# Where the high parts of expert weights are made, and where gathered rows are turned, in a decoder layer with sixteen experts

## The chip, the cores and the metric

The kernel runs on one core of a Trainium2 chip. The metric is the time of one execution on the device in microseconds (us), the median of several runs. A profile of one execution is there too; its times are in us from the start of its span unless marked ns. Engines are named as in the profile: PE is TensorE's matrix multiply, PEld its weight load, DVE is VectorE, ACT is ScalarE, POOL is GpSimd, SP is SyncE, which here only issues DMAs. A line such as L830 is a line of the kernel before.

## The reference

One layer (DEPTH = 1) over 1024 tokens of width 1024 in float32: forgetting attention with 16 heads, a residual with layer norm, then a mixture of 16 experts with a sigmoid router that gives each token two experts of one group, again a residual with layer norm.

```python
mix = forgetting_attention(h, fox_w_in[j], fox_b_f[j], fox_w_out[j])
h = _layer_norm(ALPHA * h + mix, ln1_g[i], ln1_b[i])
ffn = grouped_moe(h, router_w, router_b, moe_w_gate[i], moe_w_up[i], moe_w_down[i])
h = _layer_norm(ALPHA * h + ffn, ln2_g[i], ln2_b[i])
...
for e in range(N_EXPERTS):
    he = jax.nn.silu(hf @ w_gate[e]) * (hf @ w_up[e])
    y = y + combine[:, e:e + 1] * (he @ w_down[e])
```

Each expert has three weight matrices: gate and up of 1024 x 512, down of 512 x 1024, 2 MB each in float32.

## The kernel before

**Precision.** A float32 operand is kept as two float16 parts, high and low; a product is three matmuls (`mm3`, L93 to L97: high by high, high by low, low by high). `split` (L65) makes the parts of weights: the high part with a scaled copy on ACT (L68) or on POOL (L70), the low part as scaled source minus high part on DVE (L71). The low part is the last reader of the raw tile.

**Stages.** Value projection, then attention over eight pairs of heads, output projection with first layer norm and router (`out_units`, `route`), then the experts, then the last normalizations and the scatter of the result. Expert 0's weights are loaded during the output projection.

**The expert stage.** `JOBS` is a list of (expert, first slot, slots): expert 0 in two jobs of 80 slots, all others in one of 160, computed as a part of 128 rows and one of 32. The loop in `run` (L1331 to L1368) does for job q: `gather` of job q+1, `load_chunk` of its three weight matrices, up-projections `up` of job q for blocks f = 1 to 3, `up` of job q+1 for f = 0, `rows` of job q-1, `down` of job q.

- `load_chunk` (L757) brings a matrix in four chunks of 128 x 1024 float32 (512 KB) through five raw buffers. Tiles `mh0`, `mh1`, `mh2` are the high parts of gate, up and down, `ml0` to `ml2` the low parts; suffix a or b is the parity of the expert, so two experts' weights are held. High parts alternate between ACT and POOL (L786), except for expert 1, where all are on ACT.
- `gather` (L814) fetches a part's rows (high and low halves of 1024 columns each, float16) from DRAM by an indirect DMA from POOL into `xg`, and turns them into `xT` with the token index in the free dimension: 16 column blocks of 128. For the part of 128 rows the first eight blocks are turned by a DMA transpose issued from SP (L825); the other eight, and all 16 of the part of 32 rows, by TensorE against an identity (L829), eight blocks to a PSUM tile `xq`, and copied to `xT` by DVE (L830). The tag `tp` has two PSUM buffers.
- `up` computes gate and up products for a block of 128 hidden units (L833 to L842, 48 matmuls into `gu`), then tanh on ACT (L857), two DVE operations `a` and `t` (L858, L859), the high half of the hidden values on ACT (L860) and the low half on POOL (L861).
- `down` multiplies with the down weights; the large part is copied with its gate on ACT (`yr`, L896) and added into `acc` in DRAM by an indirect DMA from POOL (L940). The small part goes through `yl` on ACT (L930) and the sum `yT` on DVE (L931), is turned back in `rows` of the next job and added likewise.

**Order.** Each engine works through its own queue in order, and a wait holds everything behind it. The order in a queue is laid down when the program is built, from priorities, and need not be that of the text; `issue_after(ins)` asks that the instructions of its block on the engine of `ins` come behind `ins` in that engine's queue. `self.turned` holds, in the expert stage, the last copy into `xT` that `gather` issued; before, the same name also held sets of finished blocks of the attention.

Of the kernel before, what the change touches and what calls it, by code (L numbers as in the profile page):

```python
# [21 lines left out]
NT, KT, NP = S // 128, D // 128, H // 2  # L22
# [4 lines left out]
WS = 64.0  # L27
# [7 lines left out]
NA, CA, TA = 1, 80, 5  # L35
# [23 lines left out]
class Kern:  # L59
# [18 lines left out]
    def fill(self, us):  # L78
        done = 0
        while us > done and self.fill_q:  # L80

            at = next((n for n, u in enumerate(self.fill_q) if len(u) < 3 or u[2] in self.turned[NP - 1]), None)
            if at is None:
                break
            c, f = self.fill_q.pop(at)[:2]
            f()
            done += c
        return done
# [296 lines left out]
    def attn_o(self, hp, i, j, pT, ps):  # L385
        nc, wk = self.nc, self.wk
        hd = 2 * hp + j
        nb = QG if hp < NP - 1 else 1
        if i % nb == 0 and j == 0:
            self.o_ps = ps.tile([128, QG, 2, HD + 1], F32, name="ops", bufs=2)  # L390
        V = self.V[hd // 8]
        vo = hd % 8 * VW
        vh, vl = slice(vo, vo + HD + 1), slice(vo + HD + 2, vo + VW)
        o = self.o_ps[:, i % nb, j, :]
        for b in range(i + 1):
            nc.tensor.matmul(o, pT[:, b, :], V[b][:, vh], start=(b == 0), stop=False)  # L396
            nc.tensor.matmul(o[:, :HD], pT[:, b, :], V[b][:, vl], start=False, stop=False)  # L397
            nc.tensor.matmul(o, pT[:, i + 1 + b, :], V[b][:, vh], start=False, stop=(b == i))  # L398
        if j == 0 or i % nb < nb - 1:
            return  # L400
        T = self.o_ps[:, :nb]
        r = wk.tile([128, QG, 2, 1], F32, name="ro", bufs=2)[:, :nb]
        nc.vector.reciprocal(r, T[:, :, :, HD:])
        x = wk.tile([128, QG, 2, HD], F32, name="ox", bufs=1)[:, :nb]
        nc.vector.tensor_tensor(x, T[:, :, :, :HD], r.to_broadcast([128, nb, 2, HD]), op=OP.mult)  # L405
        sg = self.SG[hp, i // 4].rearrange("p (a b c) -> p a b c", b=2, c=HD)[:, (i + 1 - nb) % 4:i % 4 + 1]
        self.gated = nc.gpsimd.tensor_tensor(x, x, sg, op=OP.mult)  # L407
        gh, gl = (wk.tile([128, QG, 2, HD], F16, name=f"g{n}", bufs=2)[:, :nb] for n in "hl")
        nc.scalar.activation(gh, x, AF.Copy)
        nc.gpsimd.tensor_tensor(gl, x, gh, op=OP.subtract)  # L410
        ts = slice((i + 1 - nb) * 128, (i + 1) * 128)
        def turn():
            for g, oT in ((gh, self.oTh), (gl, self.oTl)):
                nc.sync.dma_start_transpose(oT[:, hp, ts].rearrange("p (a b) -> p a b", b=128),
                                            g.rearrange("p a b c -> p (a b c)"))
            self.turned[hp].add(i)
        self.later.append((self.now + 2, turn))

    def pairs(self, ps):
# [337 lines left out]
    def load_chunk(self, n):  # L757
        e, kind = divmod(n, 3)
        nc, I = self.nc, self.I
        if kind == 2:  # L760
            src = I["moe_w_down"][0, e].rearrange("(k p) c -> p k c", p=128)
            shape = [128, FT, D]
        else:
            src = I[("moe_w_gate", "moe_w_up")[kind]][0, e].rearrange("(k p) c -> p k c", p=128)
            shape = [128, KT, DE]
        pool, sfx = (self.p3a, "a") if e % 2 == 0 else (self.p3b, "b")
        h = pool.tile(shape, F16, name=f"mh{kind}{sfx}")
        l = pool.tile(shape, F16, name=f"ml{kind}{sfx}")
        nk = 1024 // shape[2]
        for c in range(shape[1] // nk):  # L770
            if n == 3 * NA:

                if c % 2 == 0:
                    both = self.p3b.tile([128, 2, nk, shape[2]], F32, name="raww", tag=("mh2b", "ml2b")[c // 2])
                r = both[:, c % 2]
            else:
                r = self.p3a.tile([128, nk, shape[2]], F32, name="raw", tag="raw", bufs=5)
            ks = slice(c * nk, (c + 1) * nk)
            nc.sync.dma_start(r, src[:, ks, :])
            self.sp_n += 1  # L780
            if e == NA:
                with self.tc.issue_after(self.exp.ins), self.tc.issue_after(self.indexed.ins):
                    self.split(h[:, ks, :], l[:, ks, :], r, WS, "act")
            else:
                with self.tc.issue_after(self.turned.ins) if e == 2 and 4 * kind + c >= 4 else ExitStack():
                    self.split(h[:, ks, :], l[:, ks, :], r, WS, ("act", "pool")[self.sp_n % 2 if e != 1 else 0])  # L786
        self.MW[n] = (h, l)


# [24 lines left out]
    def gather(self, job):  # L814
        nc = self.nc
        e, jo, jn = job
        xT = self.p3b.tile([128, 2 * KT, CAP], F16, name="xT", bufs=2)[:, :, :jn]
        for q, (o, n) in enumerate(self.parts(job)):
            xg = self.p3b.tile([128, 2 * D], F16, name=f"xg{q}", bufs=2)
            idx = self.idx[o]  # L820
            self.got = nc.gpsimd.indirect_dma_start(  # L821
                out=xg[:n, :], out_offset=None, in_=self.hl_d,
                in_offset=bass.IndirectOffsetOnAxis(ap=idx[:n, e:e + 1], axis=0))
            if n > 64 and e >= NA:
                nc.sync.dma_start_transpose(xT[:, :8, o - jo:o - jo + n], xg[:n, :8 * 128])  # L825
            for c in range(8 if n > 64 and e >= NA else 0, 2 * KT, 8):
                p = self.psr.tile([128, 8, n], F16, name="xq", tag="tp", bufs=2)
                for k in range(8):
                    nc.tensor.transpose(p[:, k, :], xg[:n, (c + k) * 128:(c + k + 1) * 128], self.identh[:n, :n])  # L829
                self.turned = (nc.vector.tensor_copy if e >= NA else nc.scalar.copy)(xT[:, c:c + 8, o - jo:o - jo + n], p)  # L830
        self.XT[job] = xT

    def up_mm(self, gu, job, f):  # L833
# [436 lines left out]
    def run(self):  # L1270
        tc, nc, I = self.tc, self.nc, self.I
        self.w_k = I["fox_w_in"].rearrange("a d c -> (a d) c").rearrange("(k p) c -> p k c", p=128)
        self.W, self.QA, self.SG = {}, {}, {}
        self.turned = [set() for _ in range(NP)]
        self.wo, self.OP = [None, None], {}
        self.wo_k = I["fox_w_out"].rearrange("a (k p) c -> p (a k) c", p=128)
        self.LR, self.FR, self.ROOM, self.YT, self.p2b, self.MW, self.XG, self.XT, self.sp_n = {}, {}, [], {}, None, {}, {}, {}, 0
# [107 lines left out]
```

## Time and profile before

| | |
|---|---|
| runs | 1164.64, 1170.14, 1173.2 us; median 1170.14 us |
| profiled execution | 1179.74 us, its span 1177.9 us |
| mean granted TensorE clock | 0.932 of full speed |
| busy: PE, DVE, ACT, POOL | 995.7, 798.1, 523.9, 444.1 us |
| DMA queue of SP and ACT, and of POOL | 62.3% and 10.4% of 16 engines' span |

Busy shares are means over stages with different limits; the rows below cut the expert stage out and divide it into periods, one per expert. A row of waits tells how long an engine stood idle and which instruction ended that.

### The profile page before, as it was taken

The numbers are of one execution on the slowest core, as the hardware profiler recorded it, in microseconds if no ns is written. First come the engines' busy times: TensorE is split into PE (matmuls) and PEld (weight loads), VectorE is DVE, ScalarE is ACT, GpSimd is POOL, SyncE is SP. The second block draws the span as 40 slices with busy tenths as digits, with TensorE's granted clock in tenths as the row PEclk, the third lists the DMA queues.
The fourth block names the chain that finished last, engine by engine and source line by source line (L and its number), as shares of the span: only waits on it lengthen the run. The fifth ranks groups of instructions, "written<-read, shape, count | busy, mean of one in ns | idle before, by whom it ended". The sixth has DMA issues, their size and how long they took to land. (4 is left out here: it accounts for less than half of the span.)

```text
span 1177.9 us, 27374 instructions
## 1 busy us (share of the span) xinstructions
PE 995.7 (85%) x11246; PEld 703.0 (60%) x11246; DVE 798.1 (68%) x1408; ACT 523.9 (44%) x835; POOL 444.1 (38%) x438
## 2 busy tenths in 40 slices
PE   7799799999989998978789778889789888888860
PEld 3344466575765756554344666777677767776740
DVE  3423566767667786747499768767986767777765
ACT  4111456657666575735053544433343434443431
POOL 3400421222222322123110146666665666554453
PEclk9899899999999999989899979988989999989985
DMA  8900285778678687668776479999899999998560
GB/s 247 229 19 1 53 130 110 142 131 142 126 130 155 139 166 139 121 140 149 197 253 228 164 202 304 311 278 274 246 294 262 289 265 284 280 277 258 154 204 37
DMA packets 290467, 221.77 MB, mean 188 GB/s; under 512 B 207640, under 2 KB 232216, under 8 KB 290336
## 3 DMA queue, kind: packets, MB, share of 16 engines
q1 hardware_dynamic: 281120, 188.50, 62.3%
q0 software_dynamic: 8640, 29.37, 10.4%
q8 instruction: 90, 1.47, 0.5%
q10 hardware_dynamic: 576, 2.10, 0.4%
q14 instruction: 41, 0.34, 0.1%
HBM read 147.80 MB, written 23.69 MB: 146 GB/s over the span
## 5 line engine op out<-in xcount | busy, mean ns | idle before, releaser
L379 DVE SCALAR_TENSOR_TENSOR hl<-s,hl 128x256 f16<-128x256 f32 (+7 forms) x128 | 102.0, 797 | 83.6 <-ACT hl L378 81.9
L376 ACT ACTIVATE s<-sp,mn 128x256 f32<-128x256 f32 (+7 forms) x128 | 94.3, 737 | 90.0 <-DVE mn L374 88.1
L407 POOL TENSOR_TENSOR ox<-ox,sg 128x256 f32<-128x256 f32 (+1 forms) x36 | 32.0, 888 | 252.5 <-DVE ox L405 252.5
L374 DVE TENSOR_REDUCE mn<-sp 128x1 f32<-128x256 f32 (+7 forms) x128 | 95.2, 749 | 14.5 <-PE sp L372 13.4
L95 PE MATMUL pj<-xTh,wh 128*128 128x512 f16 x256 | 97.9, 382 | 7.1 <-ACT qa L351 7.1
L378 ACT ACTIVATE hl<-s 128x256 f16<-128x256 f32 (+7 forms) x128 | 87.3, 682 | 25.8 <-DMA pT<-hl 22.9
L97 PE MATMUL pj<-xTh,wl 128*128 128x512 f16 x256 | 97.8, 382 | 0.0
L96 PE MATMUL pj<-xTl,wh 128*128 128x512 f16 x256 | 97.8, 382 | 0.0
L95 PE MATMUL pj<-wh,xTh 128*128 128x128 f16 x512 | 92.5, 225 | 1.0 <-POOL wh L70 1.0
L96 PE MATMUL pj<-wl,xTh 128*128 128x128 f16 x512 | 92.5, 225 | 0.0
L97 PE MATMUL pj<-wh,xTl 128*128 128x128 f16 x512 | 92.5, 225 | 0.0
L940 POOL DMA_INDIRECT acc<-yr,dst x29 | 56.0, 1931 | 72.1 <-DMA raw<-in_moe_w_gate_dram 26.3
L95 PEld LDWEIGHTS <-xTh 128*128 128x128 f16 x704 | 69.5, 100 | 21.5 <-DMA xTh<-xhl 3.7
L96 PEld LDWEIGHTS <-xTh 128*128 128x128 f16 x704 | 69.3, 100 | 17.9 <-issue 3.2
L97 PEld LDWEIGHTS <-xTl 128*128 128x128 f16 x704 | 69.3, 100 | 16.9 <-issue 2.6
L396 PE MATMUL ops<-v,pT 128*128 128x65 f16 x576 | 66.9, 194 | 14.0 <-DMA pT<-hl 14.0
L860 ACT ACTIVATE hh<-t 128x160 f16<-128x160 f32 (+1 forms) x68 | 22.1, 327 | 127.1 <-DVE t L859 126.8
L369 PE MATMUL sp<-kx,qa 128*128 128x512 f16 (+2 forms) x192 | 62.4, 325 | 17.5 <-ACT s L376 17.1
L396 PEld LDWEIGHTS <-pT 128*128 128x128 f16 x576 | 54.5, 98 | 29.8 <-DMA pT<-hl 19.5
L397 PE MATMUL ops<-v,pT 128*128 128x64 f16 x576 | 67.0, 196 | 0.0
L398 PE MATMUL ops<-v,pT 128*128 128x65 f16 x576 | 66.6, 194 | 0.0
L821 POOL DMA_INDIRECT xg<-hl_d,idx x31 | 49.7, 1605 | 40.2 <-DVE gsum L706 18.0
(369 smaller groups left out, 3513.9 us busy)
## 6 DMA issues: line engine op xcount, KB each, us to landing
raw<-in_moe_w_up_dram SPq DMA_DIRECT2D x64, 512.0 KB
raw<-in_moe_w_down_dram SPq DMA_DIRECT2D x64, 512.0 KB
raw<-in_moe_w_gate_dram SPq DMA_DIRECT2D x60, 512.0 KB
wr<-in_fox_w_in_dram SPq DMA_DIRECT2D x48, 256.0 KB
xr<-in_x_dram SPq DMA_DIRECT2D x8, 512.0 KB
xh<-in_x_dram SPq DMA_DIRECT2D x16, 256.0 KB
wvr<-in_fox_w_in_dram SPq DMA_DIRECT2D x6, 512.0 KB
hl_d<-hlr SPq DMA_DIRECT2D x6, 512.0 KB
```

Of the source, the lines that this page charges most:

```text
L95: nc.tensor.matmul(p, ah, bh, start=first, stop=False)
L96: nc.tensor.matmul(p, ah, bl, start=False, stop=False)
L97: return nc.tensor.matmul(p, al, bh, start=False, stop=last)
L369: nc.tensor.matmul(sp[:, ks], self.QA[hp][:, j, qb], self.KX[hp % 2][:, 2 * j, ks], start=True, stop=False)
L374: self.mn = nc.vector.tensor_reduce(mn, sp[:, :n], axis=AX, op=OP.min)
L376: nc.scalar.activation(s[:, :n], sp[:, :n], AF.Exp, scale=-1.0, bias=mn)
L378: nc.scalar.activation(hl[:, :n], s[:, :n], AF.Copy, scale=PS)
L379: nc.vector.scalar_tensor_tensor(hl[:, n:], s[:, :n], PS, hl[:, :n], op0=OP.mult, op1=OP.subtract)
L396: nc.tensor.matmul(o, pT[:, b, :], V[b][:, vh], start=(b == 0), stop=False)
L397: nc.tensor.matmul(o[:, :HD], pT[:, b, :], V[b][:, vl], start=False, stop=False)
L398: nc.tensor.matmul(o, pT[:, i + 1 + b, :], V[b][:, vh], start=False, stop=(b == i))
L940: self.nc.gpsimd.indirect_dma_start(out=self.acc, out_offset=bass.IndirectOffsetOnAxis(ap=self.dst[self.key(job, o)][:n, job[0]:job[0] + 1 ...
```

## The change

For all experts the high part of every weight chunk is made on ACT. In `gather` the DMA transpose goes; all 16 column blocks of either part are turned on TensorE, in two PSUM tiles of eight. The copies out of PSUM, four per expert, are shared: of the part of 128 rows the first on DVE and the second on ACT, of the part of 32 rows the first on ACT and the second on DVE. `issue_after(self.turned.ins)`, before for expert 2 alone (chunks from up chunk 0 on), now also holds for experts 3 to 15, for down chunks 1 to 3. The sets of the attention get a name of their own, `turns`.

```diff
@@ load_chunk
             else:
-                with self.tc.issue_after(self.turned.ins) if e == 2 and 4 * kind + c >= 4 else ExitStack():
-                    self.split(h[:, ks, :], l[:, ks, :], r, WS, ("act", "pool")[self.sp_n % 2 if e != 1 else 0])
+                with self.tc.issue_after(self.turned.ins) if e >= 2 and 4 * kind + c >= (4 if e == 2 else 9) else ExitStack():
+                    self.split(h[:, ks, :], l[:, ks, :], r, WS, "act")
@@ gather
-            if n > 64 and e >= NA:
-                nc.sync.dma_start_transpose(xT[:, :8, o - jo:o - jo + n], xg[:n, :8 * 128])
-            for c in range(8 if n > 64 and e >= NA else 0, 2 * KT, 8):
+            for c in range(0, 2 * KT, 8):
                 p = self.psr.tile([128, 8, n], F16, name="xq", tag="tp", bufs=2)
                 for k in range(8):
                     nc.tensor.transpose(p[:, k, :], xg[:n, (c + k) * 128:(c + k + 1) * 128], self.identh[:n, :n])
-                self.turned = (nc.vector.tensor_copy if e >= NA else nc.scalar.copy)(xT[:, c:c + 8, o - jo:o - jo + n], p)
+                self.turned = (nc.vector.tensor_copy if e >= NA and (c == 0) == (n > 64) else nc.scalar.copy)(xT[:, c:c + 8, o - jo:o - jo + n], p)
```

The other three hunks only rename `turned` to `turns` in `fill`, `attn_o` and `run`.

## Rows read from the trace of the kernel before

**Rows 1.** page, slices of the span; one digit for each fortieth, busy tenths
```profile
PE   7799799999989998978789778889789888888860
...
DMA  8900285778678687668776479999899999998560
```

**Rows 2.** windows of 13 expert periods: us, busy (count) by engine, clock, DMA share, GB/s
```profile
957.16:986.27 29.11, 24.55 (x315) 20.82 (x315) 20.97 (x25) 11.21 (x21) 17.30 (x15) 0.94 0.99 278
...
1044.19:1070.48 26.29, 22.34 (x312) 19.00 (x310) 20.03 (x22) 9.16 (x16) 12.79 (x10) 1.00 0.98 273
sum 375.96, PE 320.52 PEld 273.13 DVE 277.67 ACT 141.81 POOL 228.44; mean PE 24.66 PEld 21.01 DVE 21.36 ACT 10.91 POOL 17.57
```

**Rows 3.** waits of TensorE, 694 to 1071 us: total, times, longest
```profile
PE xq L829 <- DVE xT L830: 29.1, 10, 4.4
```

**Rows 4.** windows around a gap of TensorE
```profile
1002.00:1004.00 2.00, 0.71 (x13) 0.67 (x13) 1.90 (x5) 1.24 (x2) 0.00 (x0) 0.94 0.97 254
1004.00:1006.00 2.00, 2.00 (x18) 2.00 (x16) 0.77 (x2) 0.00 (x0) 0.00 (x0) 0.50 0.80 289
```

**Rows 5.** windows around three DMA transposes, and one of weights alone
```profile
962.00:965.00 3.00, 3.00 (x16) 1.34 (x15) 2.60 (x4) 1.25 (x2) 0.00 (x0) 1.00 1.32 144
990.00:993.00 3.00, 3.00 (x17) 1.51 (x16) 2.90 (x4) 1.25 (x2) 0.06 (x1) 1.00 1.23 217
1019.00:1022.00 3.00, 3.00 (x15) 1.35 (x14) 3.00 (x6) 0.47 (x2) 0.00 (x0) 1.00 1.27 119
...
1025.00:1029.00 4.00, 3.61 (x93) 3.32 (x92) 4.00 (x5) 2.42 (x5) 3.28 (x3) 1.00 1.04 397
```

**Rows 6.** groups by line, 640 to 1178 us: busy, mean ns, idle before
```profile
L71 DVE SCALAR_TENSOR_TENSOR ml2b<-raw,mh2b 128x1024 f16<-128x1024 f32 x32 | 45.1, 1437 | 27.7 <-POOL mh2b L70 21.3 <-ACT mh2b L68 6.4
...
L71 DVE SCALAR_TENSOR_TENSOR ml2a<-raw,mh2a 128x1024 f16<-128x1024 f32 x28 | 37.3, 1365 | 26.4 <-POOL mh2a L70 24.6 <-ACT mh2a L68 1.8
...
L68 ACT ACTIVATE mh2b<-raw 128x1024 f16<-128x1024 f32 x18 | 19.0, 1056 | 28.4 <-DMA raw<-in_moe_w_down_dram 25.0 <-SPq L1145 3.3
...
L70 POOL TENSOR_SCALAR mh2b<-raw 128x1024 f16<-128x1024 f32 x14 | 18.2, 1555 | 0.6 <-DMA raw<-in_moe_w_down_dram 0.6
...
L603 ACT COPY hT<-tp 128x1024 f16<-128x1024 f16 x5 | 4.9, 1014 | 4.7 <-PE tp L602 4.7
```

**Rows 7.** groups by line and form on ScalarE, 724 to 1071 us
```profile
L860 ACT ACTIVATE hh<-t 128x160 f16<-128x160 f32 x48 | 16.0, 336 | 104.3 <-DVE t L859 104.3
...
L68 ACT ACTIVATE mh2a<-raw 128x1024 f16<-128x1024 f32 x13 | 13.7, 1057 | 25.0 <-DMA raw<-in_moe_w_down_dram 25.0
...
L68 ACT ACTIVATE mh1a<-raw 128x1024 f16<-128x1024 f32 x12 | 12.6, 1049 | 6.3 <-DMA raw<-in_moe_w_up_dram 6.3
```

**Rows 8.** timeline of GpSimd, one period: start, us, instruction, idle before
```profile
978.22 1.58 POOL L940 DMA_INDIRECT acc<-yr,dst  x1 [5.48 <-DMA raw<-in_moe_w_gate_dram]
979.28 2.61 POOL L70 TENSOR_SCALAR mh2b<-raw 128x1024 f16<-128x1024 f32 x2
```

**Rows 9.** timeline of VectorE, the same period
```profile
974.28 0.88 DVE L830 COPY xT<-xq 128x1024 f16<-128x1024 f16 x2
976.44 1.23 DVE L71 SCALAR_TENSOR_TENSOR ml2b<-raw,mh2b 128x1024 f16<-128x1024 f32 x1 [1.28 <-ACT mh2b L68]
977.58 0.28 DVE L830 COPY xT<-xq 128x256 f16<-128x256 f16 x1
980.92 4.33 DVE L71 SCALAR_TENSOR_TENSOR ml2b<-raw,mh2b 128x1024 f16<-128x1024 f32 x3 [3.05 <-POOL mh2b L70]
```

**Rows 10.** timeline of SyncE's queue, the same period
```profile
973.86 10.65 SPq L779 DMA_DIRECT2D raw<-in_moe_w_gate_dram  x4
```

**Rows 11.** groups by line and form, 957.16 to 986.27 us
```profile
L829 PE MATMUL xq<-identh,xg 128*128 128x128 f16 x8 | 0.6, 219 | 0.0
```

**Rows 12.** windows of the stage that loads expert 0
```profile
600.00:620.00 20.00, 18.58 (x154) 9.04 (x152) 19.97 (x38) 11.04 (x12) 1.50 (x1) 1.00 0.75 258
```

**Rows 13.** DMA queues, 700 to 1050 us: packets, MB, share
```profile
q0 software_dynamic: 4496, 15.34, 20.8%
```

More of the change, by code (lines that the diff above doesn't have):

```diff
@@ L80, in fill @@
         while us > done and self.fill_q:
-            at = next((n for n, u in enumerate(self.fill_q) if len(u) < 3 or u[2] in self.turned[NP - 1]), None)
+            at = next((n for n, u in enumerate(self.fill_q) if len(u) < 3 or u[2] in self.turns[NP - 1]), None)
             if at is None:
@@ L415, in turn @@
                                             g.rearrange("p a b c -> p (a b c)"))
-            self.turned[hp].add(i)
+            self.turns[hp].add(i)
         self.later.append((self.now + 2, turn))
@@ L1273, in run @@
         self.W, self.QA, self.SG = {}, {}, {}
-        self.turned = [set() for _ in range(NP)]
+        self.turns = [set() for _ in range(NP)]
         self.wo, self.OP = [None, None], {}
```

## The prediction, written before the result was known

> **What bounds the kernel now.** I read the page's slices first, then windows by stage. From the 25th of the 40 slices on (about 700 us) the experts run one after another; there the DMA row stands at 9, twice at 8, up to the 37th slice, while TensorE (PE) mostly shows 8. The tail, with TensorE at 6 and then 0, is final normalization that the change does not touch [rows 1]. So the expert stage is to be priced. I cut it at the issues of the DMA transpose, one per expert: 13 periods in 375.96 us, 28.92 us each. Their sum row gives per period TensorE 24.66 busy, VectorE (DVE) 21.36, ScalarE (ACT) 10.91, GpSimd (POOL) 17.57; the DMA share is 0.99 and 0.98 in the two periods shown [rows 2].
>
> Two things are nearly full at once. The DMA engines hardly pause. TensorE has 24.66 us of work, part of it at the lower of its two clock levels: the one period with a granted clock of 1.00 needed 22.34 us and lasted only 26.29 [rows 2]. Of TensorE's idle 4.26 us per period, 29.1 us in 13 periods (2.2 each) is a wait for DVE's copy of a transposed block (xT, L830) [rows 3]; the rest, 2.0, are waits for links of the activation. No wait of TensorE names a weight tile, so weights bound the stage indirectly: their splits sit in the in-order queues of DVE, ACT and POOL ahead of the copies that TensorE does wait for. An idle gap is followed by half clock: 0.94 in the two microseconds with the gap, 0.50 in the two behind it [rows 4]. So a period is 22.34 work + 4.26 idle + 2.32 lower clock.
>
> **The change part by part.**
>
> *DMA transposes out.* Fifteen go, one per expert from expert 1 on. In three windows of 3 us around one, the DMA engines moved 144, 217 and 119 GB/s; in 4 us of weights alone 397 [rows 5]. A transpose carries 128x1024 values of 2 bytes, 0.262 MB. In the first window 0.432-0.262 = 0.170 MB of other data moved, worth 0.43 us at 397 GB/s: 2.57 us were lost. The others give 2.02 and 2.76 by the same sum. I take the mean, 2.45 us per period, and keep 2.02 and 2.76 as bounds. The first two of the fifteen lie before the periods, where I count nothing: 13 x 2.45 = 31.9 us.
>
> The Trainium skill says otherwise: its page "Advanced Engine Details and Errata", section "X-Bar Transpose (TRN2)", holds that transpose DMAs are as fast as regular ones. By that, the 0.262 MB would cost what as many bytes of weights cost. The windows speak against it, so it is only a rival below.
>
> *Splits from POOL to ACT.* POOL loses 90 high parts, six for each expert but expert 1, in groups that average up to 1.56 us; ACT gains as many at 1.06 us [rows 6]: +6.3 us per period. ACT also takes two of the four copies of transposed blocks: one 128x1024 PSUM read, nearest row 1.01 us (hT) [rows 6], and one 128x256, nearest row hh of 128x160, 0.34 [rows 7]. ACT then has 10.9+6.3+1.4 = 18.6 us of work in 26 to 29: hidden, as long as what it waits for does not add up.
>
> What the move removes is a queue effect. In one period POOL stood 5.48 us before it could issue an accumulate into acc at 978.22, and only then made two high parts of the down weights [rows 8]; DVE idled 3.05 us for them and did three low parts from 980.92 to 985.25 [rows 9]; raw buffers come free with DVE's low parts, and SP needed 10.65 us to issue four gate loads [rows 10]. Altogether DVE waited 24.6 and 21.3 us for POOL's down parts, 3.3 us per expert [rows 6]. How much of this shortens the period the trace does not show: nothing if the DMA engines stay full anyway, 3.3 at most. Below zero is possible too, since all high parts now stand in one queue with tanh and hh; the nearest price is ACT's average wait for a raw tile, 83.7 us in the six L68 rows (first and last shown) over 73 splits, 1.15 us [rows 7]. With a DMA share near 1 I stay close to zero: a gain of 0.5 us per period, 6.5 us in all.
>
> DVE's low parts also get faster. Alone an L71 takes 1.23 us; the three beside POOL took 4.33, 1.44 each [rows 9], and the six groups average 1.42 (the two for down weights 1.37 and 1.44) [rows 6]. Twelve per expert at 1.23 save 2.3 us, and one 128x256 copy goes to ACT: DVE falls to about 18.8 us. This is slack, not a term.
>
> *Eight more TensorE transposes per expert.* A group of eight 128x128 was busy 0.6 us [rows 11]. It lies beside TensorE's idle unless that vanishes, so I cost it at nothing, and raise TensorE's floor to 22.34+0.6 = 22.9. The blocks share two PSUM buffers: block 3 waits for copy 1 (DVE; two copies of 128x1024 and 128x256 took 0.88 us [rows 9]), block 4 now for copy 2 (ACT, 1.01). Best case some 1 us of waiting in all, a floor of 23.9, against 2.2 us of waiting now. The next up matmuls are queued behind these transposes.
>
> *The order edge.* For experts from 3 on, the low parts of down chunks 1 to 3 on DVE must follow the last copy. In the trace they already do: copy at 977.58, those three at 980.92 [rows 9]. I cost it at nothing; SP would pay, whose gate loads wait for those raw buffers. SP's queue loses a transpose issue and its wait for the gather.
>
> *Expert 0's load* (six splits) goes to ACT, which in that stage was busy 11.04 of 20 us while DVE was full, 19.97 [rows 12]. POOL's six splits become six of 1.06 us on an ACT with room for them: nothing, bounds -1 (DVE without POOL beside it) and +3 us (half of the six in the way).
>
> **Sum.** 2.45 + 0.5 = 2.95 us per period, 25.97 instead of 28.92; 13 periods give 38.4 us. Cross-check from TensorE: 22.9 work + 1.0 for the copies + 1.5 other idle + 0.6 lower clock = 26.0. The profiled execution took 1179.74 us, its span 1177.9; the median of the three runs is 1170.14, 9.6 lower. I take the difference off the median: 1132 us, or 1141 for a profiled one like this.
>
> **Rivals.**
> 1. *More than the sum.* The period falls to TensorE's floor, 23.9: 13 x 5.0 = 65 us, 1105. For it: a period of 26.29 us exists already, with a DMA transpose in it. Against: DMA needs 6.29 MB of weights at 397 GB/s, 15.9 us, plus the software queue's 20.8% of 350 us over 12.1 periods, 6.0 [rows 13]: 21.9 of 23.9 with five raw buffers.
> 2. *A DMA transpose costs no more than plain bytes.* Then 0.262 MB at 397 GB/s is 0.66 us; with 0.5: 13 x 1.16 = 15 us, 1155. The skill's rule named above is this one; the windows of 119 and 144 GB/s are against it.
> 3. *The wait moves, nothing is won.* Copy 1 still stands on DVE behind the sum yT, which needs ACT's yl, and ACT now has two more up parts ahead of yl. TensorE's 2.2 us for xT and the half clock stay, the freed DMA time goes unused: 1158 to 1178, about 1168. For it: copy 1 ran only at 974.28 [rows 9], when TensorE had long finished its block.
> 4. *Slower: ACT as the serial queue.* Copies 2 and 3 on ACT are queued behind high parts that wait for raw tiles, and TensorE waits for copy 2. Price: one average raw wait, 1.15, plus the 0.6 of new transposes, 1.75 x 13 = 23 us: 1193. It decides once TensorE's wait for xT per period exceeds 2.2-0.6 = 1.6 us with the clock unchanged and the DMA gain unused. For it: in twelve periods ACT waited 104.3 us for t and 83.7 for raw tiles [rows 7], 15.7 per period; with 18.6 of work that would make 34. Against: waits behind POOL's late parts are among the longest of these, and they go.
>
> **Chances.** Forecast (1110 to 1150) 0.58, rival 1 0.08, rival 2 0.08, rival 3 0.14, rival 4 0.12. A measurement of this kernel tells about 1%, 12 us, from no change. Faster by over 1%: 0.58 + 0.08 + 0.06 of rival 2: 0.72. Within 1%: the rest of rival 2 and rival 3, 0.16. Slower: 0.12. The range leaves out rival 4 and part of rival 3: 1103 to 1166. The bounds fit: the transpose's 2.02 to 2.76 move the time by +6 to -4 us, the queue effect's -1.15 to 3.3 by +21 to -36, where TensorE's floor cuts in at 1105, and expert 0's load by +3 to -1.
>
> **What will show it.** Right: periods near 26 us; no 3 us windows under 150 GB/s where the transposes were; no DVE wait for POOL at L71 and L71 near 1.23 us; TensorE's wait for xT near 1 us per period; a granted clock above 0.95. Wrong: ACT's waits for t or raw tiles grow, TensorE waits for ACT's copies of xT, or the DMA share falls with the period unchanged, which would say that the DMA engines were not the bound.

## The result and the profile after

The changed kernel takes 1127.2 us (median of 4 runs, 1124.01 to 1128.11) against 1171.67 for the kernel before (1164.64 to 1175.1): a ratio of 0.96, 95% interval 0.9568 to 0.9632. The forecast was 1132, its range 1103 to 1166. The profiled execution took 1126.3 us, its span 1124.5.

The page's slices of the kernel after. Against [rows 1], TensorE shows 9 through most of the expert stage, and the DMA row is as full as it was:

```profile
PE   7899799999999898997789978899999999989860
...
DMA  9900176678577987667768547999999999999551
```

DMA transposes no longer mark the periods, so from here on a period runs from one start of the sum yT on VectorE to the next (L931 before, L929 after), 14 of them in each kernel. Windows over these 14, kernel before; columns as in [rows 2]:

```profile
742.90:1143.00 400.10, 337.68 (x4365) 288.23 (x4364) 291.98 (x458) 154.31 (x283) 236.62 (x186) 0.92 0.91 263
```

The same of the kernel after:

```profile
734.00:1089.50 355.50, 327.01 (x4482) 279.37 (x4479) 254.77 (x443) 239.29 (x384) 137.42 (x113) 0.96 0.92 286
```

Divided by 14, the period went from 28.58 to 25.39 us. VectorE's work in it went from 20.9 to 18.2 (18.8 forecast), ScalarE's from 11.0 to 17.1 (18.6 forecast), GpSimd's from 16.9 to 9.8; the clock went from 0.92 to 0.96. Of the 53.4 us between the two profiled executions (1179.74 and 1126.3), 14 x 3.19 = 44.6 lie here. Another 8.9 lie ahead of the first period, as its start moved from 742.9 to 734.0; the profiled execution of before was itself 8 us above its median. In all eight profiled executions that make expert 0's high parts on ScalarE alone, those of the experiments below among them, the first sum comes at 732.9 to 738.9 us; in the three that alternate for all of them (742.9, 745.3 and 740.5) it comes later, and in the two that alternate for a part between (736.2 and 737.4). So some of this start belongs to expert 0's load. From the end of the periods to the end of the span it is 34.9 and 35.0.

TensorE's waits in the 14 periods after (us, times, longest). In the 14 periods before it stood 32.2 us for xT; [rows 3] has 29.1 for 13:

```profile
PE xq L827 <- DVE xT L828: 13.0, 8, 2.9
...
PE xq L827 <- ACT xT L828: 0.9, 2, 0.6
```

Groups by line after, 640 to 1124 us; they answer to [rows 6]:

```profile
L71 DVE SCALAR_TENSOR_TENSOR ml2b<-raw,mh2b 128x1024 f16<-128x1024 f32 x32 | 37.9, 1221 | 9.1 <-ACT mh2b L68 9.1
...
L71 DVE SCALAR_TENSOR_TENSOR ml2a<-raw,mh2a 128x1024 f16<-128x1024 f32 x28 | 33.5, 1222 | 6.2 <-ACT mh2a L68 6.2
...
L68 ACT ACTIVATE mh2b<-raw 128x1024 f16<-128x1024 f32 x32 | 32.7, 1055 | 8.9 <-DMA raw<-in_moe_w_down_dram 8.7
```

The waits for GpSimd are gone. For the down parts, what VectorE waits for ScalarE in their place is much less: 9.1 and 6.2 us instead of 27.7 and 26.4. For the gate parts it waits longer than before (15.9 and 12.5 us instead of 11.9 and 11.1); over all six tiles 58.2 us are left of 88.6. The low parts all take 1.22 to 1.23 us. VectorE's timeline in one period shows it, beside the gap of 3.05 us and the 4.33 us for three low parts in [rows 9]:

```profile
910.52 0.42 DVE L929 TENSOR_TENSOR yT<-yp,yl 128x256 f32<-128x256 f32 x1 [0.22 <-ACT yl L928]
910.86 0.68 DVE L828 COPY xT<-xq 128x1024 f16<-128x1024 f16 x1
911.47 1.23 DVE L71 SCALAR_TENSOR_TENSOR ml2a<-raw,mh2a 128x1024 f16<-128x1024 f32 x1
...
913.58 2.36 DVE L71 SCALAR_TENSOR_TENSOR ml2a<-raw,mh2a 128x1024 f16<-128x1024 f32 x2 [0.50 <-ACT mh2a L68]
```

ScalarE, with six microseconds more to do per period, waits less. Its waits in the 14 periods after, first for t, then for a raw tile; [rows 7] has 104.3 and 25.0 us in twelve periods:

```profile
ACT hh L858 <- DVE t L857: 31.7, 28, 2.7
...
ACT mh2a L68 <- DMA raw<-in_moe_w_down_dram: 2.6, 5, 1.0
```

Over all six rows of its high parts the wait for raw tiles went from 77.3 to 40.8 us in the 14 periods.

So the signs that the prediction named came true: periods near 26 us, no wait of VectorE for GpSimd, low parts at 1.22, a wait for xT near 1 us per period (0.9, and 0.06 more for ScalarE's copies), a clock above 0.95 in the stage. Whether they came for the reasons given is another matter.

### The profile page after: what moved, and what is told of

Same layout as the page of the kernel before. It is cut to its first block, busy times and chain, and to the rows that moved or that the text cites. A ratio compares the mean times of both kernels' runs of the same rounds, so it can differ in the third digit from the quotient of the medians.

```text
span 1124.5 us, 27572 instructions
## 1 busy us (share of the span) xinstructions
PE 988.6 (88%) x11366; PEld 698.4 (62%) x11366; DVE 751.5 (67%) x1393; ACT 625.9 (56%) x955; POOL 321.9 (29%) x348
## 5 line engine op out<-in xcount | busy, mean ns | idle before, releaser
L407 POOL TENSOR_TENSOR ox<-ox,sg 128x256 f32<-128x256 f32 (+1 forms) x36 | 31.9, 887 | 253.2 <-DVE ox L405 253.2
L859 POOL TENSOR_TENSOR hh<-t,hh 128x160 f16<-128x160 f32 (+1 forms) x56 | 54.5, 975 | 150.7 <-ACT hh L858 150.6
L95 PE MATMUL pj<-wh,xTh 128*128 128x128 f16 x512 | 92.1, 224 | 1.0 <-POOL wh L70 1.0
L938 POOL DMA_INDIRECT acc<-yr,dst x29 | 49.2, 1696 | 74.0 <-ACT mh2b L68 17.9
L95 PE MATMUL gu<-xT,mh0a 128*128 128x160 f16 (+1 forms) x288 | 58.9, 235 | 3.6 <-DVE t L857 3.6
```

Of the source, the lines that this page charges most:

```text
L95: nc.tensor.matmul(p, ah, bh, start=first, stop=False)
L859: (nc.vector if e >= E - 2 or (e < NA and jo == 0) else nc.gpsimd).tensor_tensor(hl[:, f, :], t, hh[:, f, :], op=OP.subtract))
```

## The experiments

Two readings stand against each other. The prediction's: the DMA transposes fill the engines that bound the stage, and taking them out makes most of the gain; the splits give little. Its rival: the stage waits for the split weights, GpSimd is late and slow with its high parts, and taking the splits from it makes the gain, while full DMA engines are not the bound. Each result is given with its ratio to the kernel before, run on the same chip. The kernel before has medians of 1171.67 to 1174.85 us on the chips used, so a difference in us to the kernel after, which was run apart from the experiments, is good to about 3 us.

**1. The splits alone.** All high parts go to ScalarE; DMA transposes, copies and order edge are as before.

```diff
--- after
-  with self.tc.issue_after(self.turned.ins) if e >= 2 and 4 * kind + c >= (4 if e == 2 else 9) else ExitStack():
+  with self.tc.issue_after(self.turned.ins) if e == 2 and 4 * kind + c >= 4 else ExitStack():
...
-            for c in range(0, 2 * KT, 8):
+            if n > 64 and e >= NA:
+                nc.sync.dma_start_transpose(xT[:, :8, o - jo:o - jo + n], xg[:n, :8 * 128])
+            for c in range(8 if n > 64 and e >= NA else 0, 2 * KT, 8):
...
-  self.turned = (nc.vector.tensor_copy if e >= NA and (c == 0) == (n > 64) else nc.scalar.copy)(...)
+  self.turned = (nc.vector.tensor_copy if e >= NA else nc.scalar.copy)(...)
```

> The changed kernel with the DMA transposes and DVE copies of the kernel before and without the new order edge: only the splits are moved to ACT. Theory of the prediction (the DMA transposes carry most of the gain, 31.9 of 38.4 us): about 6.5 us under the kernel before, 1165, the period near 28.4 us. Rival (POOL's late high parts are the main loss, 3.3 us per expert): 13 x 3.3 = 43 us under it, about 1129, equal to the changed kernel.

Measured: 1139.56 us, 0.9692 (0.9651 to 0.9732), 35.3 us below the kernel before. The 14 periods:

```profile
734.50:1103.40 368.90, 327.19 (x4365) 280.89 (x4364) 258.81 (x458) 227.73 (x359) 124.51 (x112) 0.94 0.96 286
```

A period is 26.35 us, 2.2 less than before, with every DMA transpose still in it. Three quarters of the gain come from the part that the prediction priced at 6.5 us.

**2. The turning alone.** TensorE turns all blocks and ScalarE makes half of the copies; high parts alternate as before.

```diff
--- after
-  with self.tc.issue_after(self.turned.ins) if e >= 2 and 4 * kind + c >= (4 if e == 2 else 9) else ExitStack():
-      self.split(h[:, ks, :], l[:, ks, :], r, WS, "act")
+  with self.tc.issue_after(self.turned.ins) if e == 2 and 4 * kind + c >= 4 else ExitStack():
+      self.split(h[:, ks, :], l[:, ks, :], r, WS, ("act", "pool")[self.sp_n % 2 if e != 1 else 0])
```

> The changed kernel with splits alternating between ACT and POOL and without the new order edge: only the turning of the column blocks is moved to TensorE. Theory of the prediction: 13 x 2.45 = 31.9 us under the kernel before, about 1140. Rival (a transpose costs what plain bytes cost, 0.66 us): 9 us under it, about 1163. If this and the splits alone add up to the 44.5 us between the two kernels, the parts are independent; if both fall short, one needs the other.

Measured: 1180.13 us, 1.0042 (1.0019 to 1.0064): no gain, half a per cent slower. The 14 periods:

```profile
745.30:1151.50 406.20, 346.66 (x4487) 295.17 (x4486) 290.13 (x443) 169.13 (x308) 222.09 (x186) 0.91 0.82 250
```

The DMA share falls from 0.91 to 0.82 and the period does not get shorter (29.01). That is the very sign for which the prediction said it would mean that the DMA engines were not the bound. What stays is TensorE's wait for the copies (32.2 us before, here 23.3 for VectorE's and 10.3 for ScalarE's) and VectorE's wait for GpSimd, 45.9 us for the two down tiles in the 14 periods before, here 56.1:

```profile
DVE ml2b L71 <- POOL mh2b L70: 28.5, 7, 5.4
DVE ml2a L71 <- POOL mh2a L70: 27.6, 6, 6.4
```

**3. Which of the splits.** In the kernel before, once only the down parts (2 of GpSimd's 6) go to ScalarE, once only gate and up (4 of 6). If the cost is the place in GpSimd's queue behind the accumulate, the first should give most of it; if it is the time that GpSimd runs beside VectorE, the second.

```diff
--- before
-  ("act", "pool")[self.sp_n % 2 if e != 1 else 0]
+  ("act", "pool")[self.sp_n % 2 if e != 1 and kind != 2 else 0]
```

> The kernel before with the high parts of the down weights alone on ACT; gate and up still alternate. It keeps 4 of the 6 POOL splits of an expert. Theory A (the loss is POOL's queue: down parts stuck behind the accumulate): most of the 35 us that the splits alone gave, 1142 to 1150. Theory B (the loss is each split beside DVE, by shared time or by POOL's slower split): a third of it, 12 us, 1160 to 1165.

```diff
--- before
-  ("act", "pool")[self.sp_n % 2 if e != 1 else 0]
+  ("act", "pool")[self.sp_n % 2 if e != 1 and kind == 2 else 0]
```

> The kernel before with the high parts of gate and up all on ACT; down still alternates. It keeps 2 of the 6 POOL splits of an expert. Theory A (POOL's queue behind the accumulate): at most 10 us of the 35, 1165 to 1175. Theory B (each split beside DVE costs): two thirds, 23 us, about 1150.

Measured: 1149.42 us, 0.9805 (0.9766 to 0.9843), and 1148.46, 0.9789 (0.9753 to 0.9825): 23.6 and 24.5 us, the same within their intervals. VectorE's waits in the 14 periods with down on ScalarE, and then with gate and up there:

```profile
DVE ml0b L71 <- POOL mh0b L70: 14.1, 6, 4.2
DVE ml0a L71 <- POOL mh0a L70: 12.8, 6, 3.4
```

```profile
DVE ml2b L71 <- POOL mh2b L70: 15.7, 6, 3.6
DVE ml2a L71 <- POOL mh2a L70: 13.3, 5, 4.6
```

Neither reading holds alone. Each half brings two thirds of the 35 us, so the halves overlap: whichever stays on GpSimd keeps a wait (3.0 and 2.1 us per period, of 5.2). That either half relieves the one queue that both share would explain it; no run shows that by itself.

**4. GpSimd busy beside VectorE, with nobody waiting for it.** In the kernel after, GpSimd scales every second high part into a tile that nothing reads. This adds work and leaves the outputs as they are.

```diff
--- after
      self.split(h[:, ks, :], l[:, ks, :], r, WS, "act")
+     e > 1 and self.sp_n % 2 and nc.gpsimd.tensor_scalar(
+         self.p3b.tile([128, 8, 128], F16, name="junk", bufs=1), ..., WS, 1.0, op0=OP.mult, op1=OP.mult)
```

> The changed kernel with a scaling of 128x1024 on POOL for every second chunk of experts from 2 on, from the high part into a tile that nobody reads: POOL is as busy beside DVE as before, but no split waits for it. Theory A (POOL's queue order was the loss): 0 to 8 us over the changed kernel, 1127 to 1135, although L71 grows to 1.4 us. Theory B (running beside DVE was the loss): 20 to 35 us more, 1147 to 1162.

Measured: 1144.44 us, 0.9765 (0.9727 to 0.9802), 17 above the kernel after and between the two forecasts. Groups by line, 640 to 1137 us:

```profile
L71 DVE SCALAR_TENSOR_TENSOR ml0b<-raw,mh0b 128x1024 f16<-128x1024 f32 x28 | 48.2, 1736 | 7.7 <-ACT mh0b L68 7.7
...
L71 DVE SCALAR_TENSOR_TENSOR ml2b<-raw,mh2b 128x1024 f16<-128x1024 f32 x32 | 42.5, 1359 | 8.3 <-ACT mh2b L68 8.3
...
L787 POOL TENSOR_SCALAR junk<-mh0b 128x1024 f16<-128x1024 f16 x14 | 23.7, 1690 | 3.7 <-ACT mh0b L68 3.3
```

The low parts, 1.22 us in the kernel after, take 1.36 to 1.74. The 14 periods:

```profile
733.90:1103.80 369.90, 328.01 (x4481) 279.24 (x4478) 301.83 (x444) 240.94 (x384) 245.35 (x189) 0.96 0.90 276
```

VectorE's work is 21.6 us per period instead of 18.2, and the period 26.42 instead of 25.39: the slower low parts are no slack, as the prediction had called them. About a third as much as their 3.4 us ends up in the period. But the slower low parts are not all of it. The extra scalings also stand in GpSimd's own queue, ahead of the low half of the hidden values (hh), for which TensorE waits. TensorE's waits in the 14 periods, here and then in the kernel after:

```profile
PE yp L886 <- POOL hh L859: 8.2, 7, 1.6
```

```profile
PE yp L886 <- POOL hh L859: 1.1, 3, 0.4
```

These 7.1 us are half of the 13.4 us by which TensorE's idle grew (28.5 to 41.9 us). No split waits for GpSimd here, but TensorE does, and the run does not part the two.

**5. A DMA transpose put back.** First the transpose of the gathered rows, into a tile that nothing reads, beside TensorE's own. It stands in SyncE's queue and waits there for the gather.

```diff
--- after
+            if n > 64 and e >= NA: nc.sync.dma_start_transpose(
+                self.p3b.tile([128, 8, 128], F16, name="xd", bufs=1), xg[:n, :8 * 128])
             for c in range(0, 2 * KT, 8):
```

> The changed kernel with the DMA transpose of the first eight column blocks added back into a tile that nobody reads; TensorE still turns all blocks. It prices the transpose (with its place in SP's queue) where the DMA engines are full and the splits no longer wait for POOL. Theory now (the splits were the limit, the transpose costs its lost transfer time only once they are out of the way): between the 12 us by which the splits alone fall short of the changed kernel and 13 x 2.45 = 31.9 us; 1139 to 1159. Rival (it costs what plain bytes cost): 9 us, 1136 or less.

Measured: 1168.35 us, 0.9963 (0.9942 to 0.9984), 41 above the kernel after: nearly the whole gain, and more than either forecast. SyncE's waits, 690 to 1040 us:

```profile
SPq L823 <- DMA xg<-hl_d,idx: 92.1, 10, 10.0
```

Ten waits of 9 us each, with the weight loads queued behind them. This mixes the transfer with the wait. A second kernel was meant to part them: it transposes a high part of the previous expert, which was taken to be long ready, again into a tile that nothing reads, 14 times.

```diff
--- after
   p = self.psr.tile([128, 8, n], F16, name="xq", tag="tp", bufs=2)
+  c == 0 and n > 64 and e > NA and nc.sync.dma_start_transpose(
+      self.p3b.tile([128, 8, 128], F16, name="xd", bufs=1),
+      self.MW[3 * (e - 1)][0][:, 0:2, :].rearrange("p a b -> p (a b)"))
```

> The changed kernel with one DMA transpose of 128x1024 per expert from 2 on that waits for nothing late: its source is the gate high part of the expert before, its target is read by nobody. It prices the transfer alone, without SP waiting for a gather. Theory (2.45 us of lost transfer time each, the DMA engines being full now): 14 x 2.45 = 34 us at most, 1150 to 1161. Rival 1 (plain bytes, 0.66 us): 9 us, 1136. Rival 2 (the DMA engines still have slack, the 41 us of the transpose that waited for its gather were SP's wait): 0 to 5 us, 1127 to 1132.

Measured: 1143.56 us, 0.9744 (0.9679 to 0.9808): 16.4 above the kernel after, 1.2 us for each transpose, and none of the three forecasts. The 14 periods:

```profile
734.10:1105.00 370.90, 332.44 (x4474) 285.25 (x4473) 256.10 (x443) 241.19 (x384) 130.16 (x113) 0.94 0.97 283
```

The source was not ready, though: the loads are issued so far ahead that the transpose reaches the head of SyncE's queue before ScalarE has made that high part. One case, the high part on ScalarE and the transpose in SyncE's queue:

```profile
879.63 2.01 ACT L68 ACTIVATE mh0b<-raw 128x1024 f16<-128x1024 f32 x2
```

```profile
880.71 1.71 SPq L825 DMA_TRANSPOSE xd<-mh0b  x1
```

SyncE's waits there, 640 to 1180 us, the first two of four rows that add up to 58.6 us:

```profile
SPq L825 <- ACT mh0a L68: 24.7, 4, 7.3
SPq L825 <- ACT mh0b L68: 15.8, 3, 6.1
```

So the 1.2 us hold a wait too, and bound what the transfer alone costs from above. The kernel with the transpose of the gathered rows has 114.8 us of such waits by the same view and takes 24.8 us longer for 56.2 us more of waiting; at that rate (an estimate) the 58.6 us of waiting alone could account for all of the 16.4 us. No run has the transfer without a wait.

What a transpose takes of the DMA engines can be read from the hardware queue (packets, MB, share), 734 to 1040 us, 12 transposes among them with the splits alone:

```profile
q1 hardware_dynamic: 44980, 77.19, 79.9%
```

and none in the kernel after:

```profile
q1 hardware_dynamic: 33375, 76.79, 73.3%
```

At the second row's rate, 76.79 MB in 0.733 x 306 = 224.3 us, the first row's 77.19 - 12 x 0.262 = 74.05 MB would take 216.3 us; it took 244.5. The other 28.2 us are 2.35 for each transpose, an estimate. The kernel of the second diff above gives 2.6 by the same sum (75.94 MB and 79.6%, 12 transposes).

**6. The small terms.** The kernel after without the order edge for experts from 3 on:

```diff
--- after
-  ... if e >= 2 and 4 * kind + c >= (4 if e == 2 else 9) else ExitStack():
+  ... if e == 2 and 4 * kind + c >= 4 else ExitStack():
```

> The changed kernel without the order edge for experts 3 to 15. Theory of the prediction: the queue order on DVE is the same without it, so 1127 us, within 3 us. Rival: without it the last low parts move ahead of the copy, TensorE's wait for xT grows by one low part of 1.22 us or more per period, 13 x 1.22 = 16 us: 1143.

With all four copies of an expert on VectorE:

```diff
--- after
-  (nc.vector.tensor_copy if e >= NA and (c == 0) == (n > 64) else nc.scalar.copy)
+  (nc.vector.tensor_copy if e >= NA else nc.scalar.copy)
```

> The changed kernel with all four copies of xT on DVE. Theory of the prediction: DVE has slack (some 18.8 of 26 us), copy 2 runs right behind copy 1, 0.68 us later, so 0 to 9 us more than the changed kernel: 1127 to 1136. Rival (sharing the copies is needed since a copy lands behind a low part of 1.22 us on DVE): 13 x (1.22 + 0.68) = 25 us more, 1152.

With the first eight transposes on TensorE made twice:

```diff
--- after
-                for k in range(8):
+                for k in list(range(8)) * (2 if n > 64 and e >= NA and c == 0 else 1):
```

> The changed kernel with the first eight transposes of the large part made twice on TensorE, 15 more groups of eight. Prediction's step (they lie beside TensorE's idle and cost nothing until its floor binds): 0 to 4 us over the changed kernel, 1127 to 1131. Rival (TensorE is the bound now): 13 x 0.6 = 8 us or more, 1135.

With expert 0's high parts alternating between ScalarE and GpSimd again:

```diff
--- after
-  self.split(h[:, ks, :], l[:, ks, :], r, WS, "act")
+  self.split(h[:, ks, :], l[:, ks, :], r, WS, ("act", "pool")[self.sp_n % 2 if e == 0 else 0])
```

> The changed kernel with the high parts of expert 0 alternating between ACT and POOL again. Prediction's step (nothing, -1 to +3 us): 1126 to 1130. Rival (the some 8 us by which the changed kernel is ahead at the first sum yT come from there): 1135.

| kernel | us | ratio, 95% interval | above the kernel after |
|---|---|---|---|
| no order edge | 1127.50 | 0.9589 (0.9550 to 0.9629) | 0.3 |
| all copies on VectorE | 1129.11 | 0.9614 (0.9564 to 0.9663) | 1.9 |
| eight transposes twice | 1128.09 | 0.9594 (0.9528 to 0.9660) | 0.9 |
| expert 0 alternates | 1130.83 | 0.9625 (0.9563 to 0.9687) | 3.6 |

All four intervals overlap that of the kernel after, so none of the four is told from it by its time alone. Nothing here is faster than it.

## Why the time was right and the reason was not

**The sum.** 2.95 us per period were forecast, 3.19 measured. But the two terms that make it up were each wrong by more than the sum was, in opposite directions: that the total came out near is luck.

**The step that failed** is this: "With a DMA share near 1 I stay close to zero: a gain of 0.5 us per period, 6.5 us in all." The splits alone gave 35.3 us, 2.2 in the period. The upper bound that stood beside it, 3.3, came from the right rows (VectorE's 24.6 and 21.3 us of waiting for GpSimd, [rows 6]) and held. The choice between the bounds was made from a mean that hides pauses. Two windows of 3 us, the one of the kernel before in which the DMA engines moved least among 100 in a row from 742.9 us on, and the same of the kernel after from 734 us on (columns as in [rows 2]), tell it better:

```profile
949.90:952.90 3.00, 3.00 (x47) 3.00 (x45) 0.55 (x1) 0.06 (x1) 3.00 (x3) 1.00 0.60 99
```

```profile
764.00:767.00 3.00, 3.00 (x42) 3.00 (x41) 2.48 (x4) 0.56 (x2) 2.40 (x2) 0.90 1.00 167
```

Before, GpSimd is busy for all of the three microseconds, VectorE and ScalarE do next to nothing, and the DMA engines run at a share of 0.60. VectorE's timeline in the kernel before shows for whom it waits:

```profile
952.35 4.33 DVE L71 SCALAR_TENSOR_TENSOR ml2a<-raw,mh2a 128x1024 f16<-128x1024 f32 x3 [5.90 <-POOL mh2a L70]
```

and SyncE's timeline that three loads take 9.66 us to be issued meanwhile:

```profile
946.28 9.66 SPq L779 DMA_DIRECT2D raw<-in_moe_w_gate_dram  x3
```

The raw tiles wait to be split, and the loads wait for the tiles. Nine of the 100 windows stand under 150 GB/s before, none after; nine with the turning alone, three with the splits alone (each from its first sum yT on). The share of 0.99 in [rows 2] did not show that, since windows over 1 ([rows 5] has 1.32) make up for those under it. By these rows and the first two experiments, the chain that set the period ran from GpSimd's high parts to VectorE's low parts, to the raw tiles, to the loads.

**The DMA transposes** were the other term, 31.9 us. As time of the DMA engines 2.45 each was about right (2.35 by the queue's rows). It was no time of the kernel: alone, their removal gave nothing (5 us the other way), and the DMA share fell instead; that the next loads waited for raw tiles and not for the engines fits this. With the splits out of the way it gives 12.4 us (from the splits alone to the whole change). So the parts do not add up: 35.3 and -5.3 alone, 44.5 together. In the kernel before, the transposes were hidden under GpSimd's lateness; taking them out is worth something only after it is gone. Whether these 12.4 us are the transfer stays open: in the 14 periods SyncE stands at the transposes until TensorE is done with earlier products, with loads behind. In the kernel before, and then with the splits alone:

```profile
SPq L825 <- PE gu L97: 15.7, 8, 4.3
```

```profile
SPq L825 <- PE gu L97: 55.9, 12, 6.9
```

The prediction named a wait of SyncE's queue and gave it no price.

The Trainium skill's page "Advanced Engine Details and Errata", section "X-Bar Transpose (TRN2)", holds that such a transpose is as fast as a regular DMA, which was rival 2's price of 0.66 us. The 2.35 us of the engines' time for 0.262 MB do not agree with it: plain weights go three to four times as fast, and the measurement decides. The 1.2 us paid in time do not decide it, since they hold SyncE's wait.

**The low parts** "slack, not a term": wrong too. GpSimd's extra work costs 17 us though no split waits for it: through low parts that take up to 1.74 us instead of 1.22, and through TensorE's longer wait for GpSimd's hh. How much of the 35 us is the slower low parts and how much is the waiting stays open: the half that has the waits behind the accumulate and the half that has more of the running gave the same, and the shares overlap.

**Right as forecast.** The order edge at nothing (0.3 us), the eight more transposes on TensorE at nothing (0.9 for eight further ones), the two copies on ScalarE without harm. Expert 0's load does not belong here: it was put between a gain of 1 us and a loss of 3, and is more likely a larger gain: putting it back costs 3.6 us, with an interval that overlaps that of the kernel after, and the first sum yT then comes 6.5 us later in the profile (740.5 against 734.0). The cross-check from TensorE held: 23.4 us busy and 2.0 idle per period, where 22.9 + 0.6 and 2.5 stood.

**The rivals.** The slower one (ScalarE as the serial queue) failed at its own premise: ScalarE's waits fell, for t from 118.9 to 31.7 us in the 14 periods, and they went with the splits: 28.8 us are left with the splits alone, 101.8 with the turning alone. "More than the sum" went the right way and stopped at 25.39 of its 23.9. That the wait only moves held for the turning by itself (32.2 us for xT before, 33.6 there), not for the whole.

## What to carry to other kernels

A mean busy share near 1 of the DMA engines is no bound: look at short windows for pauses, and at what the loads wait for in them, before pricing a transfer by its bytes. When two engines make alternate parts of one stream, price the later one by the consumer's waits for it and by how much it slows the consumer while running; here the upper bound was the better guess (2.2 of 3.3 us, where 0.5 was taken). Where two edits touch the same stall, their gains do not add: ask what each gives alone, and what it gives after the other. When an experiment is to leave a wait out, read that queue's waits in its trace before using its time.

## What the runs showed of the hardware

- A GpSimd operation on SBUF slows VectorE's two-input operation that runs beside it: 1.22 us alone, 1.36 to 1.74 beside a 128x1024 scaling on GpSimd that VectorE never waits for. The Trainium skill's page "SBUF — State Buffer", section "SBUF: two separate sides", tells of a port pair that the two share as an exclusive lock. The run agrees that one is held up by the other: (301.83 - 254.77) us of more work on VectorE over the 75 scalings of GpSimd in the 14 periods is 0.63 us for each, about two fifths of the 1.5 us that one took on average.
- A transposing DMA of 128x1024 two-byte values takes about 2.35 us of the 16 engines' time (2.6 in a second kernel), an estimate from the hardware queue's share. Its price in the kernel's time was at most 1.2 us beside a full weight stream, SyncE's wait for its source included.
- A DMA that waits in SyncE's queue holds up the loads behind it: with ten waits for a gather (92.1 us) the kernel took 41 us longer than without these DMAs, transfers included. How much of it is the wait was not measured apart.
